# Scratch of the rotation in fixed buffers and squares for the norm in the weight pool: a two-block transformer kernel

## Chip, cores and metric

One core of one Trainium2 chip. The metric is the device time of one execution in microseconds (us). The five compute queues are TensorE (PE; PEld is its weight load), VectorE (DVE), ScalarE (ACT), GpSimd (POOL) and SyncE (SP), which here only issues DMA transfers.

## What is computed

Two transformer blocks over one sequence of 512 tokens, width 1024, in float32. The first rotates queries and keys (rope), the second normalises them per head:

```python
def first_block(x, ...):
    h = rms_norm(x, ln_pre_mix)
    u_pool, q, k, v = split(h @ w_in)            # 256, 768, 768, 768 columns
    q, k = rope(q, pos), rope(k, pos)
    mix = concat([multi_scale_pool(u_pool), dilated_attention(q, k, v)]) @ w_out
    x = x + rms_norm(mix, ln_post_mix)
    f = (silu(h2 @ w_gate) * (h2 @ w_up)) @ w_down      # h2 = rms_norm(x, ln_pre_ffn)
    return x + rms_norm(f, ln_post_ffn)

def second_block(x, p, ...):
    q1, q2, k1, k2, va, qf, kf, vf, fg, qc, kc, vc = split(rms_norm(x, ln_mix) @ w_in)
    # every q and k: rms_norm over the 64 columns of each head, times a gain
    h = x + concat([diff_attention, forgetting_attention, chunk_attention]) @ w_out
    h = h + conv_gated_mlp(rms_norm(h, ln_ffn))
    return h + (p @ w_ple_proj) * sigmoid(rms_norm(h, ln_ple) @ w_ple_gate)
```

## The kernel before

Matrices are held as 128 partitions by 512 columns. Each float32 operand is split into a high part `hi` (rounded to the PE's fast format, fp32r) and a low part `lo`, and each product is made of three matmuls, hi·hi, hi·lo and lo·hi. For a weight this is done in `wunit` (L153 to L171): SP loads 128x1024 raw weights (512 KB) into the pool `raw`, which has four buffers used in strict turn; ACT writes `hi` (L165) and VectorE, or every fourth time GpSimd, subtracts it from the raw weight for `lo` (L168). The pools of `hi` and `lo` have nine buffers each.

The stages run one after the other: attention of the first block (`mix1`, to about 215 us), its feed-forward part (to about 590), attention of the second block (`mix2`, about 598 to 895), its feed-forward part and the gate. In both attention stages the work is written as a list of steps (`ORDER1`, `ORDER2`) in program order: P is a projection of queries and keys for one pair of heads (256 columns, made in two halves of 128x512, each in one PSUM bank), D in `mix2` is the first two projections at once, V a projection of values (VM, VA, VF, VC in `mix2`, with the weights w_vm, w_va and so on), T the transposes into heads, S scores with their softmax, W the weighing of the values. The framework's scheduler then puts the instructions of each engine into one fixed order, using its own estimate of when buffers and operands are free; each engine executes its own list in order and waits by semaphores for the others. So a change of buffers can move instructions of other steps. A tile of a tag (`self.slot("z")`) takes the tag's buffers in turn: z has six, m eight.

In `mix1`, each half of a projection (`out_of` in `project`) takes two z tiles: ACT copies the bank into z (L488), GpSimd makes the two crossed products with the sine in y (L493, L494), VectorE multiplies z by the cosine (L495) and subtracts and adds y (L496, L497). PE's transposes (L318, in `to_heads`) read z later, and L330 to L333 copy the heads out of PSUM.

In `mix2`, each half of a projection (`out_of` in `projected`) takes two z tiles as well: ACT copies the bank into z (L832) and writes the squares into sq (L833), VectorE sums them by head (L835), a small chain on VectorE and ACT (L838 to L845, with a logarithm and an exponential at L113) makes the factor, and GpSimd multiplies z by it (L847). sq is dead after L835. Twenty halves go through this. SP's queue carries, besides weights, the stores `gated` and `kept` of the stage's start, and the copies of head rows (`copy`, L420).

Of the kernel before, what the change touches and what calls it, by code (L numbers as in the profile page):

```python
# [9 lines left out]
F32 = mybir.dt.float32  # L10
# [5 lines left out]
P = 128  # L16
S = 512
# [6 lines left out]
WH = 524  # L24
# [38 lines left out]
class Builder:  # L63
# [388 lines left out]
    def mix1(self):  # L452
# [21 lines left out]
        tab = self.slot("m")  # L474
        nc.sync.dma_start(tab, io["tab_mult"])

        zs = {}
        ops = {}
        ps = {}
# [2 lines left out]
        def project(i):  # L482
            zs[i] = []

            def out_of(t1, ps):
                t0 = t1 - 1
                z, y = self.slot("z"), self.slot("z")
                nc.scalar.activation(z, ps, AF.Copy)  # L488
                zv, yv = [a.rearrange("p (t h d) -> p t h d", t=2, d=64) for a in (z, y)]
                cs = rot[:, t0:t0 + 2, 0:64].unsqueeze(2).to_broadcast([P, 2, 4, 64])  # L490
                sn = rot[:, t0:t0 + 2, 64:96].unsqueeze(2).to_broadcast([P, 2, 4, 32])
                a, b = slice(0, 32), slice(32, 64)
                nc.gpsimd.tensor_tensor(yv[:, :, :, a], zv[:, :, :, b], sn, ALU.mult)  # L493
                nc.gpsimd.tensor_tensor(yv[:, :, :, b], zv[:, :, :, a], sn, ALU.mult)  # L494
                nc.vector.tensor_tensor(zv, zv, cs, ALU.mult)  # L495
                nc.vector.tensor_tensor(zv[:, :, :, a], zv[:, :, :, a], yv[:, :, :, a], ALU.subtract)  # L496
                nc.vector.tensor_tensor(zv[:, :, :, b], zv[:, :, :, b], yv[:, :, :, b], ALU.add)  # L497
                zs[i].append(z)
            self.chunk("w_qk1", int(i), h, 256, out_of, i == "0", early)
# [288 lines left out]
    def mix2(self, h, rc):  # L788
# [30 lines left out]
        zs = {}  # L819
# [7 lines left out]
        def projected(i):  # L827
            out = zs[i] = []

            def out_of(t1, ps):  # L830
                z, sq = self.slot("z"), self.slot("z")
                nc.scalar.activation(z, ps, AF.Copy)  # L832
                nc.scalar.activation(sq, ps, AF.Square)  # L833
                st = self.small(8)
# [4 lines left out]
                y, w = self.small(8), self.small(8)  # L839
# [369 lines left out]
```

## Time and profile before

| | us |
|---|---|
| median of 3 runs (1320.98 to 1325.31) | 1321.66 |
| profiled execution | 1321.43 |
| its span in the trace | 1319.6 |
| PE busy (share of the span) | 1287.4 (98%) |
| VectorE busy | 926.1 (70%) |
| ScalarE busy | 713.9 (54%) |
| GpSimd busy | 141.2 (11%) |

The span is the time from the first to the last instruction. Busy shares are means over all stages, so the rows below are taken by stage. A wait is read as "engine, tile and line that waited <- engine, tile and line that released it". PE's ends are modelled: one matmul of 256 columns is drawn 0.28 us long, but the next one starts 0.12 us later.

### The profile page before, as it was taken

The numbers are of one execution on the slowest core, as the hardware profiler recorded it, in microseconds if no ns is written. First come the engines' busy times: TensorE is split into PE (matmuls) and PEld (weight loads), VectorE is DVE, ScalarE is ACT, GpSimd is POOL, SyncE is SP. The second block draws the span as 40 slices with busy tenths as digits, with TensorE's granted clock in tenths as the row PEclk, the third lists the DMA queues.
The fourth block names the chain that finished last, engine by engine and source line by source line (L and its number), as shares of the span: only waits on it lengthen the run. The fifth ranks groups of instructions, "written<-read, shape, count | busy, mean of one in ns | idle before, by whom it ended". The sixth has DMA issues, their size and how long they took to land.

```text
span 1319.6 us, 21593 instructions
## 1 busy us (share of the span) xinstructions
PE 1287.4 (98%) x7990; PEld 1145.5 (87%) x7990; DVE 926.1 (70%) x1949; ACT 713.9 (54%) x1446; POOL 141.2 (11%) x185
## 2 busy tenths in 40 slices
PE   9899989999999999999999999899999999999998
PEld 9899878988999988898899999779888888888887
DVE  7777884899999833249788878657977777633354
ACT  6466645564666633247676777645544444522241
POOL 1223220000000000000232333420000000000000
PEclk9999999999999999999999999999999999999999
DMA  7421433421333442227335443323322222322211
GB/s 253 125 68 50 112 104 104 144 96 63 118 119 102 148 156 96 96 104 241 106 90 133 135 118 101 103 104 121 128 96 96 96 97 96 104 96 96 96 49 64
DMA packets 51114, 146.00 MB, mean 111 GB/s; under 512 B 6496, under 2 KB 7392, under 8 KB 51008
## 3 DMA queue, kind: packets, MB, share of 16 engines
q1 hardware_dynamic: 51008, 144.62, 33.8%
q8 instruction: 63, 1.03, 0.3%
q14 instruction: 43, 0.35, 0.1%
HBM read 124.47 MB, written 8.39 MB: 101 GB/s over the span
## 4 chain that ended last, share of the span: by engine, by line
PE 88%; DVE 6%; ACT 2%; issue 2%; DMA 1%; POOL 1%; SPq 0%; DVEq 0%; POOLq 0%; ACTq 0%
PE p L188 22%; PE p L190 22%; PE p L189 22%; PE p L374 5%; PE p L376 5%; PE p L375 5%; PE p L285 2%; PE p L294 1%; PE p L264 1%; PE p L263 1%; PE p L293 1%; DVE sp L267 1%; DVE wl L168 1%; PE p L318 1%; PE p L399 1%
## 5 line engine op out<-in xcount | busy, mean ns | idle before, releaser
L165 ACT ACTIVATE wh<-wr 128x512 fp32r<-128x512 f32 x357 | 222.0, 630 | 296.3 <-PE p L189 261.1
L168 DVE TENSOR_TENSOR wl<-wr,wh 128x512 fp32r<-128x512 f32 x345 | 246.5, 722 | 189.0 <-ACT wh L165 177.7
L188 PE MATMUL p<-sh,wh 128*128 128x512 f32 (+1 forms) x736 | 249.0, 343 | 2.4 <-DVE sv L416 2.4
L189 PE MATMUL p<-sh,wh 128*128 128x512 f32 (+1 forms) x736 | 250.6, 343 | 0.0
L190 PE MATMUL p<-sh,wl 128*128 128x512 f32 (+1 forms) x736 | 248.2, 343 | 0.0
L374 PE MATMUL p<-wh,sh 128*128 128x256 f32 (+1 forms) x672 | 190.2, 284 | 4.1 <-ACT sz L488 1.4
L375 PE MATMUL p<-wl,sh 128*128 128x256 f32 (+1 forms) x672 | 190.0, 283 | 0.2 <-DVE wl L168 0.2
L376 PE MATMUL p<-wh,sh 128*128 128x256 f32 (+1 forms) x672 | 189.4, 284 | 0.0
L188 PEld LDWEIGHTS p<-sh,wh 128*128 128x128 f32 x736 | 137.6, 188 | 19.9 <-issue 3.0
L189 PEld LDWEIGHTS p<-sh,wh 128*128 128x128 f32 x736 | 138.4, 188 | 17.6 <-issue 0.2
L190 PEld LDWEIGHTS p<-sh,wl 128*128 128x128 f32 x736 | 137.1, 188 | 17.9 <-issue 0.5
L374 PEld LDWEIGHTS p<-wh,sh 128*128 128x128 f32 x672 | 126.5, 189 | 7.2 <-ACT sz L488 1.6
L375 PEld LDWEIGHTS p<-wl,sh 128*128 128x128 f32 x672 | 126.8, 189 | 1.2 <-DVE wl L168 0.6
L376 PEld LDWEIGHTS p<-wh,sh 128*128 128x128 f32 x672 | 126.3, 189 | 0.7 <-DVE sh L181 0.3
L189 PE MATMUL p<-sk,wh 128*128 128x512 f32 (+1 forms) x306 | 106.9, 358 | 0.4 <-DVE sk L181 0.4
L190 PE MATMUL p<-sk,wl 128*128 128x512 f32 (+1 forms) x306 | 107.2, 358 | 0.0
L188 PE MATMUL p<-sk,wh 128*128 128x512 f32 (+1 forms) x306 | 99.7, 358 | 1.7 <-ACT sk L177 1.4
L113 ACT ACTIVATE sp<-sp,m 128x128 f32<-128x128 f32 (+3 forms) x128 | 71.5, 560 | 35.7 <-DVE m L267 31.7
L188 PE MATMUL p<-so,wh 128*128 128x512 f32 (+1 forms) x246 | 88.2, 362 | 1.4 <-DVE m L267 1.0
L190 PE MATMUL p<-so,wl 128*128 128x512 f32 (+1 forms) x246 | 88.6, 360 | 0.0
L275 POOL TENSOR_SCALAR sp<-sp,m 128x128 f32<-128x128 f32 (+1 forms) x112 | 69.2, 622 | 180.5 <-DVE m L271 149.2
L189 PE MATMUL p<-so,wh 128*128 128x512 f32 (+1 forms) x246 | 88.4, 359 | 0.0
(248 smaller groups left out, 2618.9 us busy)
## 6 DMA issues: line engine op xcount, KB each, us to landing
wr<-in_w_gu SPq DMA_DIRECT2D x88, 512.0 KB
wr<-in_w_down SPq DMA_DIRECT2D x44, 512.0 KB
wr<-in_w_qk SPq DMA_DIRECT2D x31, 512.0 KB
sk<-sk SPq DMA_DIRECT2D x88, 128.0 KB
wr<-in_w_out SPq DMA_DIRECT2D x12, 512.0 KB
sv<-in_x SPq DMA_DIRECT2D x16, 256.0 KB
wr<-in_w_ple_gate SPq DMA_DIRECT2D x8, 512.0 KB
wr<-in_w_v SPq DMA_DIRECT2D x6, 512.0 KB
```

The lines of the kernel that those rows point to most:

```text
L113: i = self.nc.scalar.activation(out, in_, func, **k)
L165: nc.scalar.activation(hi[:, :w], c, AF.Copy)
L168: eng.tensor_tensor(lo[:, :w], c, hi[:, :w].bitcast(F32), ALU.subtract)
L188: mm(out, lhsT=ahi, rhs=bhi, start=start, stop=False, **more)
L189: mm(out, lhsT=ahi, rhs=blo, start=False, stop=False, **more)
L190: mm(out, lhsT=alo, rhs=bhi, start=False, stop=stop, **more)
L263: nc.tensor.matmul(ps[:, :n], lhsT=q1[:, c], rhs=k1[:, :n], start=True, stop=False)
L275: self.nc.gpsimd.tensor_scalar(p[:, :n], p[:, :n], m[:, 2:3], 1.0, ALU.mult, ALU.mult)
L285: ins = nc.tensor.transpose(pt[:, w:w + P], ps_list[qb][:, kb * P:kb * P + P], self.ident)
L374: mm(d, lhsT=h[k][0][:, a], rhs=hi[:, c], start=k == 0 and (o == 0 or not first), stop=False)
L375: mm(d, lhsT=h[k][0][:, a], rhs=lo[:, c], start=False, stop=False)
L376: mm(d, lhsT=h[k][1][:, a], rhs=hi[:, c], start=False, stop=k == 7 and (o > 0 or not first))
```

## The change

```diff
--- before.py
+++ after.py
@@ -474,6 +474,8 @@
         tab = self.slot("m")
         nc.sync.dma_start(tab, io["tab_mult"])
 
+        turned = [self.slot("m") for _ in range(2)]
+
         zs = {}
         ops = {}
         ps = {}
@@ -484,7 +486,7 @@
 
             def out_of(t1, ps):
                 t0 = t1 - 1
-                z, y = self.slot("z"), self.slot("z")
+                z, y = self.slot("z"), turned[len(zs[i]) % 2]
                 nc.scalar.activation(z, ps, AF.Copy)
                 zv, yv = [a.rearrange("p (t h d) -> p t h d", t=2, d=64) for a in (z, y)]
                 cs = rot[:, t0:t0 + 2, 0:64].unsqueeze(2).to_broadcast([P, 2, 4, 64])
@@ -828,7 +830,8 @@
             out = zs[i] = []
 
             def out_of(t1, ps):
-                z, sq = self.slot("z"), self.slot("z")
+                z = self.slot("z")
+                sq = self.wp.tile([P, 2 * WH], F32, tag="raw", name=self.nm("wr"))[:, :S]
                 nc.scalar.activation(z, ps, AF.Copy)
                 nc.scalar.activation(sq, ps, AF.Square)
                 st = self.small(8)
```

In `mix1` two tiles of the tag m are taken once and used in turn as y for all twelve halves; z then takes one tile per half. Other tiles of the tag m come two places later in its turn. In `mix2` sq is the first 512 columns of a tile of the pool `raw`, taken in turn with the weight loads; z takes one tile per half. No instruction is added, removed or changed in size. From the second edit on, lines stand two, then three further down (L833 becomes L836, L847 becomes L850). Names of buffers carry numbers, which are about ten lower in the changed kernel (p_7419 there is p_7409).

The order that the scheduler makes differs at many places. Three of them follow.

SP, start of `mix2`: the issues from w_vm's loads to those of the next projections (`in_w_qk`), before:

```order
L159 DMA wr_7334<-in_w_qk 128x1024
L1057 DMA gated<-sp_7175 128x512
L159 DMA wr_7553<-in_w_vm 128x1048
L1057 DMA gated<-sp_7185 128x512
L1057 DMA gated<-sp_7215 128x512
L159 DMA wr_7575<-in_w_vm 128x1048
L1057 DMA gated<-sp_7225 128x512
L159 DMA wr_7685<-in_w_qk 128x1024
L1057 DMA gated<-sp_7235 128x512
L1057 DMA gated<-sp_7245 128x512
L159 DMA wr_7707<-in_w_qk 128x1024
L794 DMA kept<-sv_6756 128x512
```

and now:

```order
L796 DMA kept<-sv_6754 128x512
L796 DMA kept<-sv_6756 128x512
L796 DMA kept<-sv_6758 128x512
L796 DMA kept<-sv_6760 128x512
L159 DMA wr_7543<-in_w_vm 128x1048
L159 DMA wr_7565<-in_w_vm 128x1048
L159 DMA wr_7675<-in_w_qk 128x1024
L159 DMA wr_7697<-in_w_qk 128x1024
L159 DMA wr_8090<-in_w_qk 128x1024
L159 DMA wr_8112<-in_w_qk 128x1024
L420 DMA sk_7835<-sk_7835 64x512
L420 DMA sk_7836<-sk_7836 64x512
```

The two loads of w_vm stood among the `gated` stores; they stand behind the last `kept` store, and the loads of the next projections follow them.

ACT, end of D (the last bank is p_7419, now p_7409) and the splits around it. w_vm is split into wh_7555, wh_7559, wh_7577 and wh_7581, which all stand ahead of these rows before; wh_7687 to wh_7713 are the splits for P3. Before:

```order
L833 ACTIVATE sz_7403<-p_7249 128x512
L832 ACTIVATE sz_7516<-p_7418 128x512
L165 ACTIVATE wh_7687<-wr_7685 128x512
L165 ACTIVATE wh_7691<-wr_7685 128x512
L113 ACTIVATE m_7088<-p_7082,eps 128x8
L833 ACTIVATE sz_7517<-p_7418 128x512
L113 ACTIVATE rc_7087<-m_7088 128x8
L165 ACTIVATE wh_7709<-wr_7707 128x512
L165 ACTIVATE wh_7713<-wr_7707 128x512
L113 ACTIVATE m_7393<-m_7390,eps 128x8
L113 ACTIVATE m_7393<-m_7393 128x8
L832 ACTIVATE sz_7532<-p_7419 128x512
```

and now, where wh_7545 to wh_7571 are the splits of w_vm:

```order
L113 ACTIVATE m_7383<-m_7383 128x8
L113 ACTIVATE m_7399<-m_7396,eps 128x8
L835 ACTIVATE sz_7522<-p_7409 128x512
L836 ACTIVATE wr_7523<-p_7409 128x512
L113 ACTIVATE m_7399<-m_7399 128x8
L113 ACTIVATE m_7513<-m_7510,eps 128x8
L113 ACTIVATE m_7513<-m_7513 128x8
L165 ACTIVATE wh_7545<-wr_7543 128x524
L165 ACTIVATE wh_7549<-wr_7543 128x524
L165 ACTIVATE wh_7567<-wr_7565 128x524
L165 ACTIVATE wh_7571<-wr_7565 128x524
L113 ACTIVATE m_7529<-m_7526,eps 128x8
```

The splits of w_vm stood ahead of D's third copy, and those of P3 ahead of its last; now the splits of w_vm come behind D's last copy and square, and those of P3 behind them.

ACT, between P4 and VA. The banks of P4 are p_8277 and p_8362 (now p_8267 and p_8352), those of P2, one projection earlier, p_8099 and p_8184. Before, the splits of w_va (wh_8466 and those below it, after one more that stands further up) are among P2's copies:

```order
L832 ACTIVATE sz_8168<-p_8099 128x512
L833 ACTIVATE sz_8169<-p_8099 128x512
L113 ACTIVATE sp_7914,m_7915<-sp_7914,m_7915 128x256
L113 ACTIVATE sp_7922,m_7923<-sp_7922,m_7923 128x256
L113 ACTIVATE m_8175<-m_8172,eps 128x8
L113 ACTIVATE m_8175<-m_8175 128x8
L165 ACTIVATE wh_8466<-wr_8460 128x512
L165 ACTIVATE wh_8484<-wr_8482 128x512
L165 ACTIVATE wh_8488<-wr_8482 128x512
L113 ACTIVATE sp_7933,m_7934<-sp_7933,m_7934 128x384
L113 ACTIVATE sp_7941,m_7942<-sp_7941,m_7942 128x384
L832 ACTIVATE sz_8233<-p_8184 128x512
```

and now, from the square of P4's last bank to the first split of w_va:

```order
L836 ACTIVATE wr_8402<-p_8352 128x512
L113 ACTIVATE m_8343<-m_8343 128x8
L330 ACTIVATE sk_8427<-p_8417,gq 64x512
L332 ACTIVATE sk_8428<-p_8418,gq 64x512
L177 ACTIVATE st_8582<-p_8577 128x512
L330 ACTIVATE sk_8436<-p_8417,gq 64x512
L177 ACTIVATE st_8593<-p_8588 128x512
L113 ACTIVATE m_8408<-m_8405,eps 128x8
L332 ACTIVATE sk_8437<-p_8418,gq 64x512
L113 ACTIVATE m_8408<-m_8408 128x8
L177 ACTIVATE st_8604<-p_8601 128x256
L165 ACTIVATE wh_8452<-wr_8450 128x512
```

The splits of w_va stood ahead of the copy of P2's second bank; now they stand behind the copy and square of P4's second bank and the head copies (L330, L332, L177) that follow it.

## Rows read from the trace of the kernel before

**Rows 1.** The profile's page, part 1: engine, busy us, share, instructions.

```profile
PE 1287.4 (98%) x7990; PEld 1145.5 (87%) x7990; DVE 926.1 (70%) x1949; ACT 713.9 (54%) x1446; POOL 141.2 (11%) x185
```

**Rows 2.** Waits, first 230 us, of ACT, POOL and PE: us in total, times, longest.

```profile
ACT sz L488 <- DVE sz L497: 6.2, 3, 3.8
...
POOL sz L493 <- DVE sz L497: 5.8, 2, 4.1
...
PE p L374 <- ACT sz L488: 1.4, 1, 1.4
```

**Rows 3.** Timeline at 44 us, ACT, then PE: start, us, engine, line, operation, idle before.

```profile
44.18 0.60 ACT L488 ACTIVATE sz<-p 128x512 f32<-128x512 f32 x1 [0.93 <-DVE sz L497]
...
44.83 0.39 PE L374 MATMUL p<-wh,sh 128*128 128x256 f32 x1 [1.37 <-ACT sz L488]
```

**Rows 4.** Lines of 585 to 910 us one by one: ns min/median/max, start, shape.

```profile
L165 ACT ACTIVATE wh<-wr x84: 612/632/659, 584.6 to 902.8; 128x512 fp32r<-128x512 f32 x80, 128x524 fp32r<-128x524 f32 x4
...
L168 DVE TENSOR_TENSOR wl<-wr,wh x72: 674/688/1831, 585.2 to 906.3; 128x512 fp32r<-128x512 f32 x68, 128x524 fp32r<-128x524 f32 x4
...
L833 ACT ACTIVATE sz<-p x20: 575/592/607, 618.2 to 822.3; 128x512 f32<-128x512 f32 x20
...
L113 ACT ACTIVATE sp<-sp,m x80: 385/560/731, 661.0 to 862.2; 128x128 f32<-128x128 f32 x20, 128x256 f32<-128x256 f32 x20, 128x384 f32<-128x384 f32 x20, 128x512 f32<-128x512 f32 x20
...
L113 ACT ACTIVATE m<-m,eps x20: 283/301/308, 625.8 to 825.1; 128x8 f32<-128x8 f32 x20
...
L330 ACT ACTIVATE sk<-p,gq x14: 672/682/689, 649.9 to 835.6; 64x512 fp32r<-64x512 f32 x14
...
L177 ACT ACTIVATE st<-p x48: 362/586/610, 689.4 to 885.7; 128x512 fp32r<-128x512 f32 x32, 128x256 fp32r<-128x256 f32 x16
```

**Rows 5.** Timeline of SP's DMA issues, 585 to 680 us.

```profile
592.70 0.38 SPq L159 DMA_DIRECT2D wr<-in_w_vm  x1
...
636.81 2.29 SPq L159 DMA_DIRECT2D wr<-in_w_va  x2
```

**Rows 6.** Timeline of ACT, 606 to 637 us: second and last split of w_vm.

```profile
612.05 0.64 ACT L165 ACTIVATE wh<-wr 128x524 fp32r<-128x524 f32 x1 [2.14 <-PE p L399]
...
618.67 0.64 ACT L165 ACTIVATE wh<-wr 128x524 fp32r<-128x524 f32 x1
```

**Rows 7.** Timeline of PE at VM's start, at P3's heads and at VA's start.

```profile
625.77 0.28 PE L374 MATMUL p<-wh,sh 128*128 128x262 f32 x1
625.89 0.28 PE L375 MATMUL p<-wl,sh 128*128 128x262 f32 x1
...
668.41 1.03 PE L318 MATMUL p<-ident,sz 128*128 128x128 f32 x8
...
669.53 0.48 PE L263 MATMUL p<-sk,sk 128*128 128x512 f32 x1
...
683.94 0.28 PE L376 MATMUL p<-wh,sh 128*128 128x256 f32 x1
...
686.71 0.39 PE L374 MATMUL p<-wh,sh 128*128 128x256 f32 x1 [0.34 <-ACT sz L833]
```

**Rows 8.** Windows: busy us of PE, PEld, DVE, ACT, POOL; granted clock, DMA share, GB/s.

```profile
600.00:620.00 20.00, 17.77 (x142) 16.76 (x141) 19.04 (x50) 13.71 (x33) 0.00 (x0) 1.00 0.75 256
620.00:640.00 20.00, 20.00 (x170) 20.00 (x169) 16.17 (x49) 11.54 (x28) 6.76 (x6) 1.00 0.34 109
640.00:660.00 20.00, 17.81 (x139) 15.60 (x138) 12.41 (x26) 13.28 (x26) 3.40 (x3) 1.00 0.43 121
...
820.00:840.00 20.00, 16.38 (x96) 13.51 (x95) 15.92 (x50) 15.90 (x38) 8.65 (x12) 0.91 0.31 98
```

**Rows 9.** Waits of PE, 585 to 910 us.

```profile
PE p L399 <- DVE sh L181: 1.8, 4, 0.7
...
PE p L318 <- DVE sk L331: 1.3, 1, 1.3
```

**Rows 10.** Timeline of PE at the longest stop of 700 to 850 us.

```profile
830.67 0.44 PE L263 MATMUL p<-sk,sk 128*128 128x384 f32 x1 [2.19 <-DVE m L267]
```

## Prediction

> **What bounds the kernel now.** I read the page's busy shares first: TensorE (PE) is busy 1287 us, 98% of the span [rows 1]. So only some 32 us of waiting can be won, and whatever the change does comes as PE idle time, or as its end. The next view is the waits of the first 230 us, the attention of the first block: three copies of a projection out of PSUM (L488) waited 6.2 us for a buffer that VectorE's L497 had still to release, and PE lost 1.4 us behind one of them [rows 2]. The timeline shows the place: the copy at 44.18 us is the last of the three, and the next product (values V0) needs the PSUM bank that it empties, so PE stands until 44.83 [rows 3]. Behind the other two, banks were left. The second block's attention lies at about 598 to 895 us. There a copy or a square does not wait for a z buffer at all; PE is busy 20.0 of 20 us in the window 620 to 640 and 17.8 in the one ahead of it [rows 8], and its waits are short ones on VectorE and ScalarE, 1 to 2 us a kind [rows 9]. No wait of PE for a weight split (L165 and L168) stands among them.
>
> **Part 1, the rotation's products in the first block.** Twelve products y move out of the z tag into two fixed buffers. No instruction is added or taken away. The six z buffers then hold z alone, twice as many halves as before, so the copies L488 no longer wait for L497. Worth: the 1.4 us that PE lost [rows 2, 3]. The products now wait for a y buffer to be released by L497 two halves earlier, on GpSimd's queue; GpSimd already showed 5.8 us of just such waits (L493 on L497) [rows 2], and PE stood behind none of them. Bounds: 0, if the transposes behind L493 are what is late next, and 4 us, if the three waits of ACT also fed later stops. I take 1.4, what the row of PE shows.
>
> **Part 2, the squares in the second block.** Twenty squares go from the z tag into the pool of four raw weight buffers, 512 KB each, in strict turn with the weight loads. The arithmetic is the same: 20 squares at 0.59 us on ACT, 20 sums of them on VectorE. What changes is the order. A buffer of the raw pool now serves a square between two weight loads, so a load can start only after the sum over a square has been taken, and the scheduler has placed loads and splits accordingly late. On SP's queue the two loads of w_vm, the first of them issued at 592.70 us before [rows 5], go behind all eight stores of the residual, and those of w_va, from 636.81 on [rows 5], go behind one projection more with its row copies. On ACT the last three splits of w_vm stood at 612.05 to 618.67 us [rows 6], and VM's first product ran at 625.77, 7 us later and with no gap [rows 7]. Now they stand behind the last copy and square of the first two projections (D), hence behind D's last product. ACT and VectorE work in order, so nothing can pull them forward; on SP the heads' row copies are queued behind loads that wait for squares.
>
> The price per place is: ACT's work from the last bank of one projection to the first split of the next, plus that split and its low part, less PE's own work between the two. Durations [rows 4]: split 0.63, low part 0.69 (VectorE), square 0.59 and a copy out of PSUM about the same, the norm's small logarithm 0.30 (its exponential counted alike), an exponential of the scores 0.56, a head's scaled copy (L330) 0.68, a transposed copy (L177) 0.59. PE's own: eight transposes 1.03, a 512-wide product of scores 0.48 with its second overlapping, so about 0.5 for a pair [rows 7].
> VM: copy 0.6, square 0.59, three small ones 0.9, split 0.63, low part 0.69, about 0.2 for hand-offs (an estimate): 3.6 us, and PE has one product of 0.12 to run: 3.5. In return VectorE, busy 19.04 of the 20 us ahead [rows 8], no longer does w_vm's low parts there; two of them at 0.69 bring D's end forward by 1.4. Net +2.1.
> P4: copy, square, two of 0.68, an exponential of 0.56, split, low part, hand-offs: 4.7, against 3.3 of PE work (eight transposes and three, four pairs of scores). +1.4.
> VA: copy, square, four of 0.68, three transposed copies (0.59 twice, the half-wide one 0.36), three small ones of at most 0.3, split and low part: 7.3 us. Between P4's last product and VA's first PE had 2.7 us before (683.94 to 686.71) [rows 7]; the new order puts some eight more transposes there at 0.13 each, 3.7. +3.6.
> Counted in the same way, ACT against PE: P6 7.0 against 4.5, +2.5; P7 6.7 against 3.9, +2.8; VC 6.9 against 4.7, +2.2; VF 4.1 against 4.4, which hides it but for the last transposed copy that must come first, +1.0; P2, whose first split stands only 13 PE instructions ahead, +0.5. P3, P5, P8 and P9 keep about 100 instructions or more between the last bank and their first use, at the 0.12 us from one product to the next [rows 7] some 12 us: 0.
> That is 16.1 us. From it go waits that the same order removes or that fall into these new stops: PE on the first projections' normed input (L399, 1.8) and on the heads' copies (L318, 1.3) [rows 9], 3.1. The 2.2 us stop at 830.67 behind a table [rows 10] stays.
>
> **Sum.** The profiled execution took 1321.43 us, 0.2 under the median of 1321.66, so it stands for it. 1321.4 - 1.4 + 16.1 - 3.1 = 1333.0 us, 0.9% slower. Bounds: each of the eight places is uncertain by a split and a low part, 1.3 us, according to whether PE's work between hides them. All hidden, and part 1 at its 4 us: 1321.4 - 4 + 16.1 - 10.4 - 3.1 = 1320. None hidden, and part 1 at 0: 1321.4 + 16.1 + 10.4 - 3.1 = 1345.
>
> **Rivals.** (a) The late splits are covered. The new order also moves scores and transposes into the borders, and if PE stays busy through them the eight terms shrink to about 4 us in all: 1321.4 - 1.4 + 4 - 3.1 = 1321. For it speaks that PE was busy throughout 620 to 640 us [rows 8] while scores, transposes and products took turns; against it that VM's border has only one product.
> (b) The other side, faster. In the order of before the splits are what stands in ACT's and VectorE's way: the windows 600 to 620 and 640 to 660 lack 2.2 us of PE each [rows 8]. If late splits free these queues, and the borders cost nothing, 4.4 and 1.4 go: 1315.6. It decides where a split's 0.63 and 0.69 are shorter than PE's work from the last bank on; at VM, VA and P6 the count above says that they and what is ahead of them are longer.
> (c) The clock. In the window 820 to 840 PE's granted clock was 0.91, where the other rows read 1.00, and PE stood 2.19 us there [rows 8, 10]: 9% of 20 us, as 3.6 us at the lower level (1.2 of 2.4 GHz) give, in which PE does 1.8 us less work. Were each of seven new stops of 2 us or so to take 1.8 more, the sum would be 1333 + 12.6 = 1345.6. Against it: the windows of 600 to 620 and 640 to 660 lack 2.2 us of PE and read 1.00.
> The Trainium skill, "TensorE: Matmul & The Clock Gate", section "HAM oscillation — how this bites in real kernels", says that idle gaps of PE re-throttle its clock and that half of a throttled stretch is lost. By it the stops would be paid for again, which is this rival; the row at 600 to 620, at 1.00 with as much idle time, has the better claim here.
> (d) Part 1 does not do what it says: the copies wait as before, for a z that PE has not yet transposed or a product that has no y. Then 1.4 is missing: 1334.4, within the forecast's own range.
>
> **How the numbers follow.** Forecast with its own range, 1325.6 to 1341: 0.66, (d) included. (a) 0.14, (b) 0.06, (c) 0.14. Range 1319 to 1346: it takes in both bounds and (a), and leaves (b) and the far half of (c) out, some 0.13. About 0.3%, 4 us, is what a measurement of this kernel can tell from no change, so the bounds are 1317.7 and 1325.6. Faster 0.06 is (b); same 0.15 is (a) and a little of the forecast; slower 0.79 is the rest.
>
> **What would show it.** Right: L488's wait on L497 is gone from ACT's waits; in 585 to 910 us PE's waits name the splits L165 and L168 at VM, VA, P6, P7 and VC, together 10 to 18 us; w_vm is issued after 620 us; the window 620 to 640 falls below 20.0 of PE. Wrong: PE's idle time in 600 to 900 us grows by less than 5 us (a, b), or the granted clock falls below 1.00 in several of these windows (c). L493's wait on L497 with PE's transposes behind it would be (d).

## The result: 39 us slower, all of it in the second block's attention

The changed kernel takes 1362.34 us (median), against 1323.1 of the kernel before in the same comparison: a ratio of 1.0292, 95% interval 1.0266 to 1.0318. The forecast was 1333.0, in a range up to 1346. The direction was right, the slowdown was more than three times as large.

The profiled execution took 1361.27 us with a span of 1359.5. The profile's page, part 1, of the changed kernel, against [rows 1]:

```profile
PE 1306.0 (96%) x7990; PEld 1158.8 (85%) x7990; DVE 930.2 (68%) x1949; ACT 712.6 (52%) x1446; POOL 143.2 (11%) x185
```

The same 7990 products take 18.6 us more of PE's time, so nearly half of the 40 us shows as busy time and not as waiting. The window view of the stage says the same more sharply. Columns: window, its length, busy us (and instructions) of PE, PEld, DVE, ACT and POOL, granted clock, share and GB/s of DMA. Second block's attention, before, and then changed (it ends 40 us later):

```profile
590.00:900.00 310.00, 297.46 (x2135) 273.40 (x2135) 243.18 (x673) 214.37 (x507) 89.12 (x106) 0.99 0.41 123
```

```profile
590.00:940.00 350.00, 315.56 (x2138) 286.37 (x2137) 245.09 (x674) 212.74 (x507) 91.24 (x106) 0.94 0.36 109
```

PE executes the same work (2135 and 2138 products). It is idle 310 - 297.5 = 12.5 us before and 350 - 315.6 = 34.4 us now: 21.9 us more waiting. And it is busy 18.1 us longer for that work, at a mean granted clock of 0.94 instead of 0.99. The windows of the changed kernel that answer to [rows 8], same columns:

```profile
620.00:640.00 20.00, 15.70 (x107) 15.18 (x106) 12.63 (x37) 8.64 (x21) 6.86 (x5) 0.83 0.40 138
...
660.00:680.00 20.00, 17.50 (x124) 16.44 (x124) 14.21 (x43) 13.52 (x33) 4.61 (x6) 0.91 0.38 101
680.00:700.00 20.00, 17.44 (x124) 16.75 (x124) 16.45 (x61) 13.61 (x36) 5.75 (x8) 0.91 0.11 23
700.00:720.00 20.00, 14.88 (x97) 14.24 (x98) 11.84 (x28) 9.09 (x21) 5.04 (x5) 0.74 0.46 146
820.00:840.00 20.00, 17.34 (x107) 15.56 (x106) 16.60 (x33) 13.19 (x30) 8.62 (x8) 0.83 0.27 80
860.00:880.00 20.00, 13.80 (x71) 11.31 (x70) 19.42 (x51) 16.61 (x40) 9.65 (x11) 0.74 0.56 179
```

Where the clock is below 1.00, PE ran part of the window at the lower of its two levels (1.2 of 2.4 GHz). Before, one window of this stage did so [rows 8]; now it is these six. Added up over the six stretches at the lower level (same names as above, without the instructions):

```profile
sum 41.00, PE 31.82 PEld 29.85 DVE 35.19 ACT 28.41 POOL 19.71; mean PE 5.30 PEld 4.98 DVE 5.87 ACT 4.74 POOL 3.29
```

PE worked 31.8 us at the lower level, against 3.3 before (831.7 to 835.2 us). A product of 256 columns starts 0.21 us behind the one before it there (682 to 685 us) instead of 0.12, so that the 28.5 us more hold some 13 us of loss (an estimate: 12.7 by 0.213 and 0.118 us, 14.2 if it were half). The other 4 to 5 us of PE's longer busy time are not the clock. Some 3 of them are the way in which PE's ends are drawn: the last product ahead of a stop counts as 0.28 us and not as 0.12, and PE waits 38 times in the stage instead of 20 (an estimate, 18 times 0.16 us). The rest is open. PE's waits in the stage (total, times, longest), against [rows 9]:

```profile
PE p L285 <- DVE st L178: 7.4, 4, 3.1
PE p L374 <- ACT wh L165: 7.3, 4, 3.4
PE p L294 <- DVE st L178: 5.1, 7, 2.0
PE p L263 <- DVE m L267: 3.7, 8, 1.1
PE p L374 <- DVE sk L333: 2.2, 1, 2.2
PE p L375 <- DVE wl L168: 1.8, 5, 0.9
```

The timeline of PE shows the stops one by one, with the time idle ahead of each in brackets. VM's start, the stretch ahead of VA and VA's start, and the end of the stage:

```profile
626.79 0.74 PE L374 MATMUL p<-wh,sh 128*128 128x262 f32 x3 [3.37 <-ACT wh L165]
628.46 0.59 PE L375 MATMUL p<-wl,sh 128*128 128x262 f32 x1 [0.93 <-DVE wl L168]
...
701.00 0.44 PE L285 MATMUL p<-ident,sp 128*128 128x128 f32 x2 [3.06 <-DVE st L178]
...
708.29 0.80 PE L374 MATMUL p<-wh,sh 128*128 128x256 f32 x2 [2.98 <-ACT wh L165]
...
866.72 0.58 PE L294 MATMUL p<-st,sv 128*128 128x256 f32 x1 [2.04 <-DVE st L178]
...
870.67 0.66 PE L285 MATMUL p<-ident,sp 128*128 128x128 f32 x2 [2.52 <-DVE st L178]
872.63 1.76 PE L318 MATMUL p<-ident,sz 128*128 128x128 f32 x7 [1.30 <-POOL sz L850]
```

The signs of late splits came, if weaker than told: PE waits for splits (L165, L168) at VM, VA, P6 and P7, together 9.1 us where 10 to 18 was told, but at VC the releaser is another, and w_vm is issued at 617.63 us, late, though not after 620. Most of the other waits are for L178 on VectorE (the low part of the transposed weights of the scores). At VM the row of ACT shows the splits behind D's last square, as the new order has them:

```profile
623.95 0.59 ACT L836 ACTIVATE wr<-p 128x512 f32<-128x512 f32 x1
...
625.67 0.30 ACT L113 ACTIVATE m<-m,eps 128x8 f32<-128x8 f32 x1 [1.03 <-DVE m L841]
...
626.12 2.21 ACT L165 ACTIVATE wh<-wr 128x524 fp32r<-128x524 f32 x4
```

Two places cost far more than told. The first is VA. Ahead of it PE stood 3.06 and 1.15 us, at transposes that need L178's result. On VectorE that stands behind copies of two heads (L331, L333):

```profile
699.61 0.73 DVE L333 SCALAR_TENSOR_TENSOR sk<-p,gq,sk 64x512 fp32r<-64x512 f32 x1
700.27 0.67 DVE L178 TENSOR_TENSOR st<-p,st 128x512 fp32r<-128x512 f32 x1
```

Before, three of these transposes (L285) stood ahead of VA's first product at 686.71 us [rows 7] and the next among its products, at 692.84; now fifteen stand ahead of it, and PE has nothing else to run. VA itself then cost 2.98 us more, since SP issued w_va only at 703.89 us (636.81 before [rows 5]) behind the row copies of the heads, and ACT waited 5.18 us for it. SP's issues, then the split on ACT:

```profile
617.63 4.78 SPq L159 DMA_DIRECT2D wr<-in_w_vm  x2
...
695.63 4.93 SPq L420 DMA_DIRECT2D sm<-sm  x8
700.66 3.17 SPq L420 DMA_DIRECT2D sk<-sk  x4
703.89 1.08 SPq L159 DMA_DIRECT2D wr<-in_w_va  x2
```

```profile
707.61 1.15 ACT L165 ACTIVATE wh<-wr 128x512 fp32r<-128x512 f32 x2 [5.18 <-DMA wr<-in_w_va]
```

The second is the end of the stage. At 864 to 873 us VectorE did seven low parts of the output weights in the middle of the last heads' work, with the transposed weights that PE was waiting for in between (VectorE's timeline, same columns):

```profile
863.97 2.36 DVE L168 TENSOR_TENSOR wl<-wr,wh 128x512 fp32r<-128x512 f32 x2
866.25 0.41 DVE L178 TENSOR_TENSOR st<-p,st 128x256 fp32r<-128x256 f32 x1
...
870.45 1.23 DVE L168 TENSOR_TENSOR wl<-wr,wh 128x512 fp32r<-128x512 f32 x1
```

The first two took 2.36 us, where one takes 0.69 [rows 4]; GpSimd did a low part of its own beside them (864.34 to 865.78 us), and why they were slow was not tested.

In the first block part 1 did what it says. ACT's wait of L488 (now L490) on the subtraction is gone from its list, and GpSimd's wait for a y buffer fell to one of 2.9 us, against 5.8 in [rows 2]:

```profile
POOL sm L495 <- DVE sz L498: 2.9, 1, 2.9
```

PE is 1.2 us ahead of the kernel before at 140 us, and has lost it by 166: at 159 to 162 us the clock fell behind a stop that is in both kernels. Experiment 1 shows that place.

### The profile page after: what moved, and what is told of

The parts are those of the page before. It is cut to its first block, busy times and chain, and to the rows that moved or that the text cites. A ratio compares the mean times of both kernels' runs of the same rounds, so it can differ in the third digit from the quotient of the medians.

```text
span 1359.5 us, 21570 instructions
## 1 busy us (share of the span) xinstructions
PE 1306.0 (96%) x7990; PEld 1158.8 (85%) x7990; DVE 930.2 (68%) x1949; ACT 712.6 (52%) x1446; POOL 143.2 (11%) x185
## 3 DMA queue, kind: packets, MB, share of 16 engines
q8 instruction: 63, 1.03, 0.3%
## 4 chain that ended last, share of the span: by engine, by line
PE 84%; DVE 9%; ACT 3%; DMA 1%; issue 1%; SPq 1%; POOL 0%; DVEq 0%; ACTq 0%; POOLq 0%
PE p L188 21%; PE p L189 21%; PE p L190 21%; PE p L375 5%; PE p L374 5%; PE p L376 5%; DVE wl L168 2%; PE p L285 1%; DVE sp L267 1%; PE p L294 1%; ACT sp L113 1%; PE p L263 1%; PE p L293 1%; PE p L264 1%; DVE sk L331 1%
## 5 line engine op out<-in xcount | busy, mean ns | idle before, releaser
L165 ACT ACTIVATE wh<-wr 128x512 fp32r<-128x512 f32 x357 | 219.4, 629 | 294.2 <-PE p L189 261.4
L168 DVE TENSOR_TENSOR wl<-wr,wh 128x512 fp32r<-128x512 f32 x345 | 245.8, 722 | 181.6 <-ACT wh L165 170.8
L188 PE MATMUL p<-sh,wh 128*128 128x512 f32 (+1 forms) x736 | 249.5, 344 | 2.4 <-DVE sv L416 2.4
L374 PE MATMUL p<-wh,sh 128*128 128x256 f32 (+1 forms) x672 | 194.1, 293 | 10.9 <-ACT wh L165 7.3
L375 PE MATMUL p<-wl,sh 128*128 128x256 f32 (+1 forms) x672 | 194.6, 291 | 2.0 <-DVE wl L168 1.8
L376 PE MATMUL p<-wh,sh 128*128 128x256 f32 (+1 forms) x672 | 191.4, 287 | 0.0
L188 PEld LDWEIGHTS p<-sh,wh 128*128 128x128 f32 x736 | 137.9, 189 | 20.0 <-issue 3.0
L190 PEld LDWEIGHTS p<-sh,wl 128*128 128x128 f32 x736 | 137.5, 189 | 18.1 <-issue 0.5
L374 PEld LDWEIGHTS p<-wh,sh 128*128 128x128 f32 x672 | 130.1, 195 | 14.4 <-ACT wh L165 9.3
L375 PEld LDWEIGHTS p<-wl,sh 128*128 128x128 f32 x672 | 130.8, 195 | 4.8 <-DVE wl L168 4.2
L376 PEld LDWEIGHTS p<-wh,sh 128*128 128x128 f32 x672 | 130.6, 195 | 0.9 <-DVE sh L181 0.3
L188 PE MATMUL p<-sk,wh 128*128 128x512 f32 (+1 forms) x306 | 99.8, 358 | 1.6 <-ACT sk L177 1.4
L188 PE MATMUL p<-so,wh 128*128 128x512 f32 (+1 forms) x246 | 88.4, 362 | 1.4 <-DVE m L267 1.0
```

Of the source, the lines that this page charges most:

```text
L165: nc.scalar.activation(hi[:, :w], c, AF.Copy)
L168: eng.tensor_tensor(lo[:, :w], c, hi[:, :w].bitcast(F32), ALU.subtract)
L188: mm(out, lhsT=ahi, rhs=bhi, start=start, stop=False, **more)
L190: mm(out, lhsT=alo, rhs=bhi, start=False, stop=stop, **more)
L374: mm(d, lhsT=h[k][0][:, a], rhs=hi[:, c], start=k == 0 and (o == 0 or not first), stop=False)
L375: mm(d, lhsT=h[k][0][:, a], rhs=lo[:, c], start=False, stop=False)
```

## Experiments

All ratios are to the kernel before, measured beside each run. My theory: the squares' turns in the raw pool make weights and splits late, and PE pays in stops and in a lower clock behind them. The rivals: the y buffers of part 1 cost it; four raw buffers are too few for what now goes through them; the late loads alone do it, without the splits' place on ACT.

| run | median us | ratio, 95% interval |
|---|---|---|
| changed | 1362.34 | 1.0292, 1.0266 to 1.0318 |
| 1 part 1 alone | 1320.74 | 0.9981, 0.9965 to 0.9997 |
| 2 part 2 alone | 1363.95 | 1.0302, 1.0281 to 1.0323 |
| 3 two squares in one raw buffer | 1337.38 | 1.0104, 1.0080 to 1.0129 |
| 4 only D's squares in raw | 1327.06 | 1.0013, 1.0001 to 1.0025 |
| 5 w_va first | 1362.52 | 1.0290, 1.0262 to 1.0318 |
| 6 weights asked for behind each projection | 1362.73 | 1.0281, 1.0263 to 1.0298 |
| 7 fill in three stops | 1362.65 | 1.0278, 1.0260 to 1.0297 |
| 8 part 1, fill at U0 | 1322.68 | 0.9979, 0.9965 to 0.9993 |
| 9 five raw buffers | 1360.65 | 1.0275, 1.0253 to 1.0296 |
| 10 before, five raw buffers | 1319.61 | 0.9961, 0.9947 to 0.9975 |
| 11 part 1, three raw buffers | 1324.11 | 0.9993, 0.9976 to 1.0009 |
| 12 weights asked for ahead of the squares | 1328.59 | 1.0021, 1.0008 to 1.0035 |
| 13 part 1, weights asked for early | 1320.53 | 0.9965, 0.9948 to 0.9981 |
| 14 part 1, five raw buffers | 1316.19 | 0.9929, 0.9913 to 0.9944 |

### 1 and 2: each part alone

```diff
 # 1: squares back in z                          # line 833 of the changed kernel
-                z = self.slot("z")
-                sq = self.wp.tile([P, 2 * WH], F32, tag="raw", name=self.nm("wr"))[:, :S]
+                z, sq = self.slot("z"), self.slot("z")
 # 2: rotation's products back in z
-        turned = [self.slot("m") for _ in range(2)]
-                z, y = self.slot("z"), turned[len(zs[i]) % 2]
+                z, y = self.slot("z"), self.slot("z")
```

> Part 1 alone: the rotation's products in two m tiles, the squares back in the z tag. Theory A (the whole slowdown comes from the squares taking turns in the raw weight pool, which makes the weights late): within 2 us of the kernel before, 1320 to 1325, with the wait of L488 on the subtraction gone and about 1 us gained in the first 140 us. Theory B (the two m tiles or a changed turn of the tags carry part of it): more than 8 us above the kernel before.

> Part 2 alone: squares in the raw weight pool, the rotation's products back in the z tag. Theory A: the time of the changed kernel within 4 us, 1358 to 1367, and in the second block's attention the same stops of PE behind weight splits and the same falls of the granted clock. Theory B: below 1352.

The forecast's account of the two parts held, the size of the second did not: part 1 alone is 0.2% faster than the kernel before, part 2 alone has the whole loss. Its stage looks like that of the changed kernel (columns as in the window views above, here and in all that follow):

```profile
590.00:940.00 350.00, 317.27 (x2162) 288.95 (x2161) 247.34 (x679) 212.98 (x509) 94.73 (x106) 0.94 0.37 111
```

Part 1 gains less than it could. Window 156 to 166 us, with a stop of PE behind the values' low part (L416) in each: before, then part 1 alone, where that work comes 1.6 us earlier:

```profile
156.00:166.00 10.00, 7.64 (x37) 6.11 (x36) 9.55 (x22) 6.88 (x16) 3.35 (x4) 1.00 0.50 150
```

```profile
156.00:166.00 10.00, 7.70 (x27) 6.18 (x28) 8.05 (x19) 5.34 (x11) 2.41 (x4) 0.83 0.35 101
```

The stop is 2.36 us before and 2.37 with part 1. The clock stays at 1.00 in the one and falls to 0.83 of the window in the other, and the 1.5 us that part 1 had won are gone. That belongs to the executions profiled more than to the change: the same stop, 2.36 to 2.43 us, is in fifteen of the sixteen kept traces, and the low level comes with it in twelve; the kernel before is one of the three others. Nor is the 0.2% won in the first block. In the two profiles the lead is nil at 323 us and 2.4 us at the end of the second block's attention, most of it made behind 820 us, where the stop at 830.67 [rows 10] is 1.18 us instead of 2.19 and the clock stays at 1.00 (829.15 in part 1 alone). So the gain is measured, and its cause is not shown.

### 3 and 4: fewer squares in the pool

```diff
 # 3: both halves of a projection in one raw buffer
+            both = []
-                sq = self.wp.tile([P, 2 * WH], F32, tag="raw", name=self.nm("wr"))[:, :S]
+                if not both:
+                    both.append(self.wp.tile([P, 2 * WH], F32, tag="raw", name=self.nm("wr")))
+                sq = both[0][:, (t1 // 2) * S:(t1 // 2) * S + S]
 # 4: only the first two projections
+                sq = (self.wp.tile([P, 2 * WH], F32, tag="raw", name=self.nm("wr"))[:, :S]
+                      if i in "01" else self.slot("z"))
```

> The changed kernel with both halves of a projection's squares in one raw weight buffer, so that the squares take 10 turns of the pool instead of 20. Theory A (each turn holds back a weight load): the slowdown of 39 us shrinks by a third to two thirds, 1335 to 1350. Theory C (the scheduler's order in any case puts the splits behind the squares, and the number of turns does not matter): within 5 us of the changed kernel.

> The changed kernel with only the four squares of the first two projections (D) in the raw weight pool, the other sixteen back in the z tag. Theory F (each place pays for itself; VM's stop and its clock cost 4.3 + 3.4 us less the 2 us that the stage's start gains): 4 to 7 us above the kernel with part 1 alone, 1325 to 1328. Rival (a late start of the weights is carried on through all later places): more than 12 us above it.

Both in the range told. With ten turns instead of twenty the ratio is 1.0104; against part 1 alone that is 1.2% of 3.1%. PE is idle 17.9 us and busy 303.1 in the stage, between the kernels before and changed in both:

```profile
590.00:911.00 321.00, 303.12 (x2137) 276.85 (x2137) 244.69 (x674) 211.85 (x507) 92.60 (x106) 0.98 0.40 119
```

With D's four squares alone the ratio is 0.3% above part 1 alone, some 4 us, and VM's stop is the same 3.37 us as in the changed kernel. Later places are not touched in their stops (P2's are 1.32 and 0.87 us, as before the change): each place pays for itself.

```profile
631.17 0.63 PE L374 MATMUL p<-wh,sh 128*128 128x262 f32 x3 [3.37 <-ACT wh L165]
```

### 5 and 6: asking for the weights earlier, but behind the squares

```diff
+        ahead = {}
+        def load(i):                 # a new step L of ORDER2
+            u = range(2) if i.isupper() else range(2 * int(i), 2 * int(i) + 2)
+            ahead[i] = {j: self.wunit("w_v" + i.lower() if i.isupper() else "w_qk2", j) for j in u}.get
 # project and values take get=ahead.get(...); ORDER2:
-    ... F P2 T3 P4 T2 VA W00 ...
+    ... F P2 T3 LA P4 T2 VA W00 ...                                  # 5
+    ... P3 L2 T1 T0 S00 S01 F P2 L4 T3 P4 LA T2 VA L5 W00 ...        # 6, and so on to L9
```

> The changed kernel with the two loads of w_va and their splits asked for one projection earlier (ahead of P4), so that on SP's queue they stand ahead of the row copies of the heads behind which they were issued at 703.89 us. Theory D (SP's queue holds the load back: ACT waits 5.2 us for w_va at 707.6, and PE's stops of 698 to 708 us and the half clock to 712 follow from it): 6 to 12 us below the changed kernel, 1350 to 1356, ACT's wait for w_va below 1 us, the window 700 to 720 at a granted clock above 0.9. Rival (the stop only moves, since VA's splits or the next weights wait as long in another place): within 4 us of the changed kernel.

> The changed kernel with the weights of each projection from P2 on, and of VA, VF and VC, asked for in the program right behind the projection ahead of it instead of at their use, so that the scheduler ranks loads and splits ahead of the heads' and scores' work in between. Theory G (the order, not the number of buffers, makes them late): more than half of the 39 us comes back, below 1343. Theory A (four buffers, of which squares hold up to two, are too few): 1355 to 1365.

Both expectations of a gain failed in the total. In 5 the place itself did what was told. The changed kernel, 740 to 770 us, and then the run, 700 to 720 and 740 to 770 (700 to 720 of the changed kernel is among the windows above, 14.88 busy at 0.74):

```profile
740.00:770.00 30.00, 25.84 (x178) 22.15 (x177) 25.64 (x79) 21.59 (x56) 8.76 (x12) 1.00 0.41 134
```

```profile
700.00:720.00 20.00, 20.00 (x170) 19.67 (x169) 15.96 (x41) 13.79 (x31) 3.76 (x4) 1.00 0.38 107
740.00:770.00 30.00, 25.76 (x172) 23.67 (x173) 24.68 (x62) 20.59 (x46) 11.26 (x12) 0.89 0.38 114
```

The stops and the low clock of 700 to 720 are gone. In the profiled executions the lead is 7 us at 735 us and 3 us at the end: stops come up to 764 us that were not there and the clock falls behind them, 0.89 where it was 1.00. The medians are equal (1362.52 and 1362.34). In 6, which leaves VM's weights where they were, VM's 3.37 us stayed, and so did 3.06 and 1.15 at the transposes ahead of VA. VA's own stop of 2.98 went, since w_va was issued at 701.31 us, ahead of four row copies (sk) behind which it stood; but VF's stops grew from 0.41 and 0.55 to 0.51, 1.06 and 1.02 us, and the clock fell at 744 and 802 us too, where it had not. The difference: in 5 w_va was asked for ahead of P4, and so ahead of P4's squares; in 6 all weights from P2 on were asked for behind the squares of the projection ahead of them.

### 7 and 8: work for PE in the stops

```diff
 # in chunk, ahead of the first product of VM, P2 and VA (7); in pool_in, ahead of U0, into a bank of scores (8: 20 times)
+                    for _ in range(24):
+                        mm(ps[0][:, :256], lhsT=h[7][1][:, 0:P], rhs=h[7][0][:, 0:256], start=True, stop=True)
```

The added products compute nothing that is used; the first real product overwrites them.

> The changed kernel with 24 extra products of 256 columns (24 x 0.12 = 2.8 us of PE work, overwritten at once) ahead of the first product of VM, of P2 and of VA, where PE stood 3.37, 2.20 and 2.98 us. Theory E (the stops themselves cost about half, the other half is the clock that falls behind them: 3.4, 1.7 and up to 5 us at 1.2 GHz): with PE at work in the stops the granted clock stays at 1.00 at 627 to 634 and 661 to 665 us, and the time falls by 4 to 8 us in spite of the added work, 1354 to 1358. Rival (the clock does not hang on the stops): the falls stay and the time is the same or up to 3 us longer.

> Part 1 alone, with 20 extra products of 256 columns (2.4 us) ahead of the slab U0, where PE stands 2.37 us with and without part 1. With part 1 the clock fell behind that stop (159 to 162 us) and took back the 1.5 us gained before it. Theory E: the clock stays at 1.00 there and the time is 1 to 2 us below part 1 alone. Rival (the fall comes anyway, or the extra products lengthen the stop): the same as part 1 alone or up to 2 us longer.

At VM the clock did as told, the total did not follow. Window 626 to 636 us, changed and filled:

```profile
626.00:636.00 10.00, 8.28 (x45) 7.97 (x46) 8.47 (x18) 5.51 (x12) 5.82 (x4) 0.66 0.42 141
```

```profile
626.00:636.00 10.00, 8.45 (x68) 8.04 (x67) 7.78 (x19) 6.52 (x15) 4.86 (x4) 1.00 0.51 160
```

With PE at work ahead of VM the clock stays at 1.00 instead of 0.66; of the stops of 3.37 and 0.93 us, 0.51 and 1.04 are left. At VA it stays too (700 to 720 us: 1.00 instead of 0.74), but the order of PE changed with the fill: the stops of 3.06 and 1.15 us at the transposes are not there, one of 1.69 at 693 us is, and so this place does not test the fill alone. At P2 the added products could not run in the stop, since the stop is a wait for the bank, not for weights (L334, L333 without the added lines, copies the heads out of it), and they only came on top; the clock fell there as before. PE's timeline at P2 and VA:

```profile
661.79 4.60 PE L372 MATMUL p<-sh,sh 128*128 128x256 f32 x24 [2.20 <-DVE sk L334]
...
703.68 3.12 PE L372 MATMUL p<-sh,sh 128*128 128x256 f32 x24
```

By 740 us the filled kernel has made good 4.6 us against the changed one. Between 585 and 760 us its stops of 0.3 us and more sum to 11.2 us instead of 18.8, and the low clock took 3.4 instead of 11.9 (the sum of 1 - clock over windows of 1 us); against these 7.6 and 8.5 stand 3.03 + 4.60 + 3.12 = 10.75 us of added products. But it came to 585 us 3.2 us late. In the first block, which the edit does not touch, the clock fell behind two stops that the changed kernel has too, of 1.57 and 1.62 us, with its clock at 1.00 throughout; in the filled one they are 2.00 and 1.62. Windows of changed and filled:

```profile
50.00:70.00 20.00, 16.86 (x130) 15.79 (x131) 13.69 (x44) 12.34 (x32) 4.58 (x9) 1.00 0.33 91
```

```profile
50.00:70.00 20.00, 16.54 (x102) 15.52 (x103) 11.16 (x35) 9.71 (x25) 2.95 (x6) 0.83 0.33 90
```

Some 2 us more went after 760 us, where a fall was added at 801 (0.84 and 0.43 us of stops, the same in both). So the profile shows a gain at the place and a loss of about the same size elsewhere. Only one execution is profiled; that the others lost it at the same places is not shown.

At U0 (8) the clock also stays at 1.00 with the fill, against 0.83 in part 1 alone,

```profile
156.00:166.00 10.00, 8.73 (x61) 7.51 (x60) 9.68 (x23) 8.99 (x22) 1.49 (x3) 1.00 0.48 144
```

but the fill itself waited 1.26 us for its bank, and its twenty products then took 2.5 us. From the start of the stop to the end of the next one of 1.0 us (L188) it is 22.8 us, against 23.0 in part 1 alone and 21.4 before. The first eight of the twenty:

```profile
162.01 1.21 PE L534 MATMUL p<-sh,sh 128*128 128x256 f32 x8 [1.26 <-DVE m L267]
```

What follows: at VM the low clock hung on the stop, the one place where a fill shows it cleanly. At U0 the clock also stayed up in three executions without a fill, so that one filled execution there proves little. Where the fill waited for the same bank as PE, at P2, it held nothing up.

### 9, 10 and 11: the number of raw buffers

```diff
 # 9 (changed), 10 (before), 14 (part 1 alone): five raw buffers, room from the split weights
-NW = 9
+NW = 8
-        raw = self.wp.tile([P, 2 * WH], F32, tag="raw", name=self.nm("wr"))
+        raw = self.wp.tile([P, 2 * WH], F32, tag="raw", name=self.nm("wr"), bufs=5)
 # 11 (part 1 alone): bufs=3, NW stays 9
```

> The changed kernel with five raw weight buffers instead of four; the room is taken from the split weights (eight pairs instead of nine). Theory A (too few raw buffers: squares hold one or two of four, so weights are loaded and split only as squares are summed): the time in the second block's attention comes down by a third or more of its 40 us, total 1335 to 1352. Rival G2 (turns among the squares decide, not how many buffers there are): within 5 us of the changed kernel, 1357 to 1367.

> The kernel before with the same five raw buffers and eight pairs of split weights: the control for the run with five. Both theories: within 8 us of the kernel before; the difference between the two runs is what squares in the raw pool cost with five buffers.

> Part 1 alone, squares in z, but with three raw weight buffers instead of four in the whole kernel: fewer buffers without squares among them. Theory A: the second block's attention becomes slower too, by 5 to 20 us against part 1 alone, with weight splits standing later. Rival G2 (a load that waits for a square's sum is what hurts, not the number): less than 4 us there.

The rival of too few buffers fell, in both directions. Five buffers leave 1360.65. Three buffers without squares among them cost no more than a few us in the whole kernel, against 39. In the run with five, w_vm was issued at 613.83 us instead of 617.63, and VM's stop did not shrink by that: it is 3.38 us, since the splits stand on ACT behind D's last square as before.

```profile
613.83 2.35 SPq L159 DMA_DIRECT2D wr<-in_w_vm  x2
```

```profile
625.95 0.63 PE L374 MATMUL p<-wh,sh 128*128 128x262 f32 x3 [3.38 <-ACT wh L165]
```

So neither the number of buffers nor the arrival of w_vm decides there, but the place of the splits in ACT's order.

### 12 and 13: asking for the weights ahead of the squares

```diff
-    "G0 G1 D VM H P3 T1 T0 S00 S01 F P2 T3 P4 T2 VA W00 T4 S10 W01 N0 P5 S11 W10 S20 W11 P6 N1 T5 VF "
+    "G0 G1 LD LM D VM H L3 L2 P3 T1 T0 S00 S01 F L4 P2 T3 LA P4 T2 VA W00 T4 S10 W01 N0 L5 L6 P5 S11 W10 S20 W11 LF P6 N1 T5 VF ..."
 # and so on: L8 L7 P8, LC P7, L9 LE P9 (E: the three loads of w_out2a)
```

> The changed kernel, four raw buffers and squares among them, but the weights of every projection are asked for in the program ahead of the squares of the projection before it (as w_va was in the run with w_va first), so that no load's turn in the raw pool stands behind a square that PE has not yet made. Theory H (turns: the pool's buffers are given out in program order, so a load cannot be placed ahead of the squares of the projection before it, however many buffers there are): w_vm is issued before 600 us again, its splits stand ahead of D's end, and two thirds or more of the 40 us come back, 1320 to 1337. Rival A (squares simply take up buffers): above 1345.

> Part 1 alone (squares in z) with the same early asking for weights: the control. Both theories: within 6 us of part 1 alone, 1315 to 1327; the difference to the run with squares in the raw pool is what the squares still cost when no turn of a load stands behind them.

The theory of the order of asking held. With four buffers, and with all twenty squares among them, the time is 1328.59: of the 3.1% between part 1 alone and the changed kernel 0.4% is left, and 0.56% against its own control (1.0021 against 0.9965). w_vm is issued before 600 us again, and the stage has 16.0 us of idle and 303.0 of busy PE:

```profile
595.80 0.38 SPq L157 DMA_DIRECT2D wr<-in_w_vm  x1
```

```profile
590.00:909.00 319.00, 303.01 (x2156) 280.91 (x2155) 246.34 (x678) 212.43 (x508) 92.60 (x106) 0.97 0.40 121
```

The remaining 0.56% was not followed further; the trace of this run has single stops of 2.20, 2.22 and 2.09 us at 659, 813 and 841 us with a low clock behind them (0.67, 0.66 and 0.83 over 10 us).

### 14: the version that comes out best

> Part 1 with five raw buffers and eight pairs of split weights, squares in z: the two steps that each came out a few tenths of a per cent below the kernel before. If they add, 0.4 to 0.8% below the kernel before, 1314 to 1319; if both are the chance of where the clock falls, within 0.3% of it.

Part 1 with five raw buffers, squares in z, is 0.71% faster than the kernel before (0.9929, 0.9913 to 0.9944), and so faster than both. The two gains add, within the intervals; why five buffers help by 0.4% was not followed. Its stage has 8.3 us of idle PE, against 12.5 before:

```profile
590.00:898.00 308.00, 299.71 (x2173) 278.23 (x2172) 239.40 (x672) 217.21 (x512) 91.30 (x106) 0.99 0.42 128
```

## Why the forecast was too small, step by step

**Part 1**: -1.4 told. The waits that it removes are gone, and PE gains 1.2 us to 140 us in the changed kernel and 1.6 in part 1 alone. Both lose it again, in the profiled executions, to a fall of the clock that no step of the forecast had. Alone, part 1 is still 0.19% (0.03 to 0.35) faster, but the profile has that lead in the second block, not at the waits that part 1 removes (experiment 1); that the sign came out as told is luck.

**Part 2, mechanism**: right, and shown by experiments 2, 4 and 12: weights become late, ACT's splits stand behind the squares of the projection ahead, PE stops at the border. What makes them late was told only in part. "A load can start only after the sum over a square has been taken" is not the limit at VM (experiment 9: an earlier load, the same stop). The turn in the pool is what decides: weights asked for behind squares stand behind them in the order, with four buffers or five (9), at their use or right behind the projection (6, where only VA's own stop went); asked for ahead of them they do not (12, and w_va in 5). That the scheduler hands out the turns of a pool in program order is inferred from these four runs; no row of a trace shows it.

**Part 2, the terms**: VM 3.5 told, 3.37 + 0.93 = 4.3 measured. P6 2.5 told, 0.68 + 1.21 + 0.57 = 2.5. VF 1.0 and 0.41 + 0.55 = 1.0. VC 2.2 and 0.34 + 0.36 + 1.45 = 2.2. P7 2.8 and 0.84 + 0.42 + 0.35 = 1.6. P4 1.4 and 0.47 + 1.12 = 1.6. P2 0.5 told; its stop grew from 0.87 to 2.20, but behind the heads' copy L333, not behind the splits. That several agree is partly luck. Splits are what PE waits for at VM, at VA's own stop, in 0.57 us of P6 and in the last two of P7; P4's stops are behind the scores (L267), those of VF and VC behind L177, L178 and L298. And at VM ACT's instructions start 0.48 us apart where the sum took 0.6 each, but ACT stood 1.03 us for the norm's chain on VectorE (L841), which the sum does not have. Two terms failed. VA: 3.6 told (by the durations that the step lists ACT's part adds up to 7.7 and not 7.3, so 4.0), 3.06 + 1.15 + 2.98 = 7.2 measured. The step counted ACT's queue alone, from P4's last bank to VA's first split. It let PE run its transposes in that time, but PE stood 4.2 us at them, behind VectorE; and it took the load of w_va as there, though it had named w_va as late on SP: it came 5.18 us after ACT was free for it. And the end of the stage was given nothing, though the output weights go through the same pool: 2.04 + 2.52 + 1.30 = 5.9 us where VectorE does their low parts in one bunch. Together 9.5 us; the idle time grew by 21.9 where 16.1 - 3.1 = 13.0 was told.

**The clock**: this miss is about as large as that of the waits. It was priced at 0 in the sum and at 12.6 in rival (c), with a chance of 0.14; it cost some 13 us of PE's 18.1, and the forecast's own sign for (c), a clock below 1.00 in several windows, came. The step that failed is the evidence against (c): the windows 600 to 620 and 640 to 660 lack 2.2 us of PE each at a clock of 1.00 [rows 8]. In the first those are short stops, the longest 0.7 us, nearly all behind the normed input (1.8 by [rows 9]), with products in between; in the second they are one of 1.3 [rows 9] and one of 0.87. They say little of one stop of 2 us or more, for which the trace of before had one row in this stage, 830.67, and behind it the clock had fallen [rows 8, 10]. The nearest row in the stage was the one that spoke for the rival. It was no proof either: in the first block the same trace has a stop of 2.36 us with the clock at 1.00 (experiment 1). In the changed kernel's stage every stop of 2 us or more has a low clock behind it or around it, and so have two shorter ones (1.12 us at 680 and 1.45 at 825). The price itself was near: six falls instead of seven, and where stops came in pairs, the low level lasted on. In 700 to 720 us it took 0.26 of 20 us, 5.2 us at most (PE did not work in all of it), and as much in 860 to 880.
The Trainium skill, "TensorE: Matmul & The Clock Gate", section "HAM oscillation — how this bites in real kernels", says of idle gaps, longer than most of those here, that they re-throttle PE and that half of each throttled stretch is lost beside the idle time itself. The windows at VM agree: granted 0.66 over 626 to 636 us behind a stop of 3.37, and 1.00 there once PE had work in the stop (experiment 7). The shorter stops that the clock fell behind are this case's own finding.

**Rivals**: (a) and (b) were wrong. At P4, VF and VC no split held PE up, as (a) has it, but stops of about the size counted came there all the same, behind other work of VectorE and ScalarE; and nothing came free that showed. (d) was wrong. (c) was right as a mechanism and near in size, with six windows below 1.00; added to the forecast's stops it gave 1345.6. The two missed terms, 9.5, and the 4 to 5 us of PE's busy time that are not the clock bring that to some 1360, against 1361.27 of the profiled execution; this takes them from the result, and so it is an account and no test.

## What to carry to other kernels

A scratch tile in a pool whose buffers go round in program order is not free because its size fits: here every prefetch asked for behind the scratch in that pool stood behind the work that writes it. Ask for the prefetch ahead of it in program order, or keep the pools apart; more buffers alone did not help here.
When a forecast adds stops of PE of 1 to 3 us, give the low clock behind each a price and a chance: here 21.9 us of added waiting came with some 13 us lost to it.
Read the idle time of a window with its pieces beside it: a sum of many short stops says little about one long one.

## What was not expected of the hardware

The same stop of 2.36 and 2.37 us, at the same instruction, left the clock at 1.00 in the kernel before and took it to 0.83 of a 10 us window in part 1 alone (experiment 1); of fifteen kept traces with this stop, twelve show the low level with it. So a gain of that size upstream can be lost at a later stop that was harmless, and two versions that differ by 1 or 2 us of waiting may come out the same. The length of a stop alone did not tell either: in the changed kernel 1.12 us at 680 was followed by a low clock and 1.57 and 1.62 in the first block were not, while in experiment 7 stops of 2.0 and 1.62 us at the same places of the first block were.
